# Half of the top-k counts moved from VectorE to GpSimd and ScalarE in a two-layer sparse-attention and retention trunk

## The chip, the cores and the metric

The kernel runs on one core of a Trainium2 chip. Its metric is device time in microseconds (us) of one execution. The engines named below are TensorE (PE), VectorE (DVE), ScalarE (ACT), GpSimd (POOL) and SyncE (SP, which issues the DMAs); each works through its own list of instructions in order.

## The reference, cut to what matters

Input and output are 1024 tokens of 1024 features, float32. Layer 0 is sparse attention: an indexer scores all keys, each query keeps the 256 best admissible keys, and attention runs over those. Layer 1 is retention. A gated convolutional feed-forward layer follows each.

```python
def block(args):                          # 8 blocks of 128 queries
    qb, qib, wb, tb = args
    limit = (tb // CHUNK + 1) * CHUNK
    admissible = key_pos[None, :] < limit[:, None]
    rel = relu(einsum('bqhd,bsd->bqhs', qib, ki))
    score = einsum('bqhs,bqh->bqs', rel, wb)
    score = where(admissible[None], score, -inf)
    _, idx = lax.top_k(score, 256)
    logits = einsum('bqhd,bqkd->bqhk', qb, gather(k, idx))
    p = softmax(where(valid, logits, -inf))
    return einsum('bqhk,bqkd->bqhd', p, gather(c, idx))
y = concat(blocks) @ w_out                # then conv_ffn, then retention, then conv_ffn
```

## The kernel before, in words

Every float32 product is made of three matmul passes over a high and a low part: `whi`/`wlo` for weights (L87 on ACT, L89 on DVE or, where the table of weights says so, on POOL), `hh`/`hl` and `qh`/`ql` for inputs. `bank` is one PSUM bank of 512 columns. A weight is fetched into `wraw` and split two weights ahead; three `whi`/`wlo` buffers go round.

Layer 0 is worked in two halves of four query blocks of 128. Block b has 128(b+1) keys, so blocks 0 and 1 need no top-k, blocks 2 to 7 have 384, 512, 640, 768, 896 and 1024 keys. The order is: `in_proj(0)`; the indexer for blocks 2 and 3 (relu on ACT, L385 adds the heads on DVE into `sc`); `in_proj(1)` with the indexer for blocks 4 to 7 inside it; attention for blocks 0 to 3; `out_proj(0)`; the first products of the feed-forward layer (`first_products`, 17 of the 22 chunks, copied out by ACT at L787); attention for blocks 4 to 7; `out_proj(1)`; the rest of the feed-forward layer.

The top-k finds each query's 256th largest score bit by bit. A count (L405) compares a block's scores with the threshold `tkt` and adds up the ones in `tkc`; two small steps turn the counts into the next threshold (L415, L416) and one keeps the best so far (L417). There are 33 counts for each block. Then L422 to L428 turn `sc` into an additive mask (a scan ranks ties). Two such searches exist: one for blocks 2 and 3, one for blocks 4 to 7; each works on all its blocks in one round. Their steps are generators, called by `steps(n)` between the pieces of other work.

Attention is made in groups of four heads. `att_probs` makes scores with the mask added and the row maximum (L484), the exponent's bias (L489), the exponential on ACT (L491), the reciprocal of its sum (L474) and the scaling on POOL (L475). `att_values` transposes the probabilities on PE (L512) and multiplies. One group is prepared ahead of the values.

The order within each engine's list is made by a scheduler when the kernel is built, which takes the program's order as the priority; it is fixed before the kernel runs.

Of the kernel before, what the change touches and what calls it, by code (L numbers as in the profile page):

```python
# [51 lines left out]
class Prog:  # L52
# [59 lines left out]
    def small(self, n, dt=F32):  # L112
        return self.sp.tile([128, n], dt, tag=f"s{n}", bufs=6 if n <= 8 else 2, name=f"s{n}")
# [102 lines left out]
    def in_proj(self, half, hh, hl, steps, also=lambda j, q, qs: None):  # L216
# [42 lines left out]
        for j in range(4):  # L259
            pq = self.proj_T(hh, hl, q0)  # L260
            sq = squares(pq[:, q0:])
            self.later(1, lambda j=j, sq=sq: sums(pms[:10, q0:], ea(2 + j), sq, False, j == 3))
            th, tl = self.tmp(F32R), self.tmp(F32R)
            self.split_psum(th[:, q0:], tl[:, q0:], pq[:, q0:], self.col(C_GQI))
            for (dst, src) in ((qs[0:64, 2 * j], th[0:64, q0:]), (qs[64:128, 2 * j], tl[0:64, q0:]),
                               (qs[0:64, 2 * j + 1], tl[64:128, q0:]), (qs[64:128, 2 * j + 1], th[64:128, q0:])):
                nc.sync.dma_start(dst.bitcast(F32), src.bitcast(F32))
            steps((2, 10)[half])
# [56 lines left out]
        self.later((4, 3)[half], idx_keys)  # L325
# [65 lines left out]
    def topk(self, scs, scratch):  # L391
# [3 lines left out]
        V = self.nc.vector  # L395
        B = len(scs)
        Ls = [sc.shape[1] for sc in scs]
        sml = lambda n, dt=F32: self.stat.tile([128, B], dt, tag=f"k{n}{B}", name=f"tk{n}")
        cnt, need = sml("c"), sml("n")
        best, bit, thr = sml("s", I32), sml("b", I32), sml("t", I32)  # L400
# [9 lines left out]
        yield from count(lambda b: 0.0, ALU.is_ge)  # L410
        V.tensor_scalar(best, cnt, TOPK - 0.5, -1.0, op0=ALU.is_lt, op1=ALU.mult)
        V.tensor_scalar(thr, best, 1 << 30, None, op0=ALU.bitwise_xor)
# [5 lines left out]
        yield from count(lambda b: t[:, b:b + 1], ALU.is_gt)  # L418
        V.tensor_scalar(need, cnt, -1.0, float(TOPK), op0=ALU.mult, op1=ALU.add)
        for b in range(B):  # L420
            nth, eq = scratch[:, 0, :Ls[b]], scratch[:, 1, :Ls[b]]
            V.tensor_scalar(eq, scs[b], t[:, b:b + 1], None, op0=ALU.is_equal)  # L422
            V.tensor_tensor_scan(nth, eq, eq, 0.0, ALU.add, ALU.max)
            yield
            V.scalar_tensor_tensor(eq, nth, need[:, b:b + 1], eq, op0=ALU.is_le, op1=ALU.mult)
            yield
            V.scalar_tensor_tensor(scs[b], scs[b], t[:, b:b + 1], eq, op0=ALU.is_gt, op1=ALU.add)
            V.tensor_scalar(scs[b], scs[b], -1.0, -MASKED, op0=ALU.add, op1=ALU.mult)  # L428
            yield

    def attention(self, blocks, q, masks, get_ot):

        items = [(b, g) for b in blocks for g in range(2)]
        nxt = self.att_probs(*items[0], q, masks)
        for _ in nxt:
            yield
        for n, (b, g) in enumerate(items):
            lg = self.lg
            ahead = self.att_probs(*items[n + 1], q, masks) if n + 1 < len(items) else iter(())
            nk = b + 1  # L440
            done = 0
            for j, _ in enumerate(self.att_values(b, g, lg, *get_ot())):
                while done < 5 and done * (nk + 1) < AHEAD * (j + 1):
                    next(ahead, None)
                    done += 1
                yield
            for _ in ahead:
                pass

    def att_probs(self, b, g, q, masks):  # L450
# [13 lines left out]
        else:  # L464
            if b == 0 and g == 0:
# [4 lines left out]
        last = None  # L470

        def normalise(i, sm):
            rs = self.small(1)
            nc.vector.reciprocal(rs, sm)  # L474
            nc.gpsimd.tensor_scalar(lg[:, i, :nk * 128], lg[:, i, :nk * 128], rs, 1.0, op0=ALU.mult, op1=ALU.mult)  # L475

        for i in range(4):
            h = 4 * g + i
            mx = []
            for (o, n) in self.segs(L):  # L480
                ps = self.bank()
                self.mm3(ps[:, :n], qh[:, h], ql[:, h], self.kTh[:, o:o + n], self.kTl[:, o:o + n], True, True)
                m = self.small(1)
                nc.vector.tensor_tensor_reduce(lg[:, i, o:o + n], ps[:, :n], mask[:, o:o + n], 1.0,  # L484
                                               mx[-1] if mx else INADM, ALU.add, ALU.max, m)
                mx.append(m)
            s = self.sq[:, b, h:h + 1]
            nm = self.small(1)
            nc.vector.scalar_tensor_tensor(nm, mx[-1], -1.0, s, op0=ALU.mult, op1=ALU.mult)  # L489
            sm = self.small(1)  # L490
            nc.scalar.activation(lg[:, i], lg[:, i], AF.Exp, bias=nm, scale=s, accum_out=sm)  # L491
            if last:
                normalise(*last)
            last = (i, sm)
            yield
        normalise(*last)
        yield

# [64 lines left out]
    def retention(self, half, x, h=None, then=None, also=lambda n: None):  # L563
        nc = self.nc
        hh, hl = h or self.all_chunks(x, C_GMIX + 8)
        kz = self.stat.tile([128, 4, 4], F32, tag="kz", name="kz")
        kn = self.stat.tile([128, 4, 4], F32, tag="kn", name="kn")
        ke = self.stat.tile([128, 4, 4], F32, tag="ke", name="ke")
# [237 lines left out]
    def second_inputs(self, x0, x1, tt, chunk):  # L806
# [3 lines left out]
        for k in (0, 2):  # L810
# [3 lines left out]
            self.split(two(T1, 0, k), two(T1, 1, k), two(x0, k))  # L814
        for k in range(4):
# [22 lines left out]
    def ffn_first(self, x, tt, s3):  # L838
# [5 lines left out]
        nxt = self.prep_b(0, 0, self.up_raw(0, 0), s3)  # L844
        T1, T2, T4, B22, T3 = self.second_inputs(x0, x1, tt, chunk)
# [45 lines left out]
    def ffn_whole(self, l, x):  # L891
# [38 lines left out]
        nxt = self.prep_b(l, 0, wa[0][0], s3)  # L930
        T1, T2, T4, B22, T3 = self.second_inputs(x0, x1, tt, chunk)
# [125 lines left out]
    def run(self):  # L1057
# [5 lines left out]
        with ExitStack() as es:  # L1063
# [27 lines left out]
            with tc.tile_pool(name="og0", bufs=2, reuse_waits="tile") as self.ogp, \  # L1091
# [54 lines left out]
                q0, qs0 = self.in_proj(0, *h0[:2], steps)  # L1146
                steps(100)
                self.sc = l0.tile([128, 4224], F32, tag="sc", name="sc")
                for b in (2, 3):
                    for _ in self.indexer(b, qs0, (b - 2) * 128, masks):  # L1150
                        pass
                    self.flush(self.nproj + b - 1)
                self.mean_square(1)
                scratch = l0.tile([128, 2, 1024], F16, name="scratch")
                gens.append(self.topk([masks[2], masks[3]], scratch))
                idx = []

                def index(j, q, qs):
                    if j == IDX_FROM:
                        idx.append((None for b in (4, 5, 6, 7) for _ in self.indexer(b, qs, (b - 4) * 128, masks)))  # L1160
                    if j >= IDX_FROM:
                        for _ in range(-(-32 // (8 - IDX_FROM))):
                            next(idx[0], None)

                q1, qs1 = self.in_proj(1, *h1[:2], steps, index)
# [13 lines left out]
                for _ in self.first_products(range(NFF - PRE[0]), B):  # L1179
                    steps(3)  # L1180
# [120 lines left out]
```

## Time and profile before

| | |
|---|---|
| median of 3 runs | 2787.89 us (2786.62 to 2789.54) |
| the profiled execution | 2782.56 us, span 2780.8 us |
| PE busy | 2654.3 us (95%) |
| DVE busy | 1881.0 us (68%) |
| ACT busy | 1090.9 us (39%) |
| POOL busy | 264.9 us (10%) |

How to read it: the page divides the span in 40 slices. PE stands at 9 tenths in nearly all of them after the first ten, so the stretch in which PE is not full is the first quarter, up to some 713 us. There DVE shows 9 tenths in the slices from about 140 to 560 us, while PE shows 7 and 6. PEclk, the clock that TensorE was granted, falls to 7 tenths in the slices where PE waits most. POOL works almost only in that first quarter.

### The profile page before, as it was taken

Reading aid. Unit: us, or ns where it says so; the run is one execution under the profiler, and the core shown is the slowest. Engines: PE = TensorE matmul, PEld = TensorE weight load, DVE = VectorE, ACT = ScalarE, POOL = GpSimd, SP = SyncE. Lnnn points to the kernel's source line nnn. Section 1 sums busy time; section 2 is a strip of 40 time slices with the busy share of each in tenths; the row PEclk is TensorE's granted clock in tenths of the full one; section 3 lists DMA queues with packets and bytes.
Section 4 is the critical chain, followed back from the end, with each engine's and each line's share of the span. In section 5 each row is a group of like instructions: output and inputs, shape, how many; then the busy total and the mean of one; then the engine's idle time right before and its main releaser. Section 6 shows DMA issues by size and latency. Waiting matters only on the chain.

```text
span 2780.8 us, 31488 instructions
## 1 busy us (share of the span) xinstructions
PE 2654.3 (95%) x11888; PEld 2175.0 (78%) x11888; DVE 1881.0 (68%) x2928; ACT 1090.9 (39%) x1546; POOL 264.9 (10%) x193
## 2 busy tenths in 40 slices
PE   8977679998999999999999999999998999999999
PEld 6755568787788878888888888888886888888887
DVE  5699999975987878744444445445447977777632
ACT  6435423563433333323333333323334554544210
POOL 2443234321000000000000000000000000000000
PEclk9988789999999999999999999999999999999999
DMA  6220025304466575412222224222222432337722
GB/s 196 71 78 23 31 91 172 116 5 152 163 200 195 195 257 177 152 61 96 84 77 90 91 77 128 76 82 92 80 73 90 144 106 106 120 108 288 232 59 87
DMA packets 110344, 328.35 MB, mean 118 GB/s; under 512 B 12400, under 2 KB 13808, under 8 KB 110192
## 3 DMA queue, kind: packets, MB, share of 16 engines
q1 hardware_dynamic: 110192, 326.34, 35.7%
q8 instruction: 93, 1.52, 0.2%
q14 instruction: 59, 0.48, 0.1%
HBM read 250.27 MB, written 72.35 MB: 116 GB/s over the span
## 4 chain that ended last, share of the span: by engine, by line
PE 77%; DVE 4%; DMA 2%; ACT 1%; issue 1%; POOL 0%; SPq 0%; DVEq 0%; ACTq 0%
PE bank L731 28%; PE bank L123 16%; PE bank L125 16%; PE bank L124 16%; PE bank L512 1%; DMA gin<-ud 1%; DMA wraw<-in_wf_up 1%; DVE T L709 1%; DVE xo L742 1%; DVE wlo L709 1%; PE bank L688 0%; DVE t L742 0%; DVE x L717 0%; DMA ud<-cu 0%; DVE gin L742 0%
## 5 line engine op out<-in xcount | busy, mean ns | idle before, releaser
L87 ACT ACTIVATE whi<-wraw 128x1024 fp32r<-128x1024 f32 (+1 forms) x194 | 204.9, 1056 | 510.3 <-PE bank L124 263.0
L731 PE MATMUL bank<-T,whi 128*128 128x512 f32 x1072 | 336.8, 395 | 21.9 <-ACT T L708 14.8
L731 PE MATMUL bank<-B,whi 128*128 128x512 f32 x1056 | 326.4, 392 | 7.7 <-DVE B L709 4.0
L89 DVE TENSOR_TENSOR wlo<-wraw,whi 128x1024 fp32r<-128x1024 f32 (+1 forms) x151 | 184.6, 1224 | 209.0 <-ACT whi L87 207.9
L124 PE MATMUL bank<-g,whi 128*128 128x512 f32 x704 | 273.6, 389 | 0.0
L125 PE MATMUL bank<-g,wlo 128*128 128x512 f32 x704 | 272.1, 389 | 0.5 <-DVE wlo L709 0.5
L123 PE MATMUL bank<-g,whi 128*128 128x512 f32 x704 | 265.5, 390 | 5.6 <-ACT g L708 4.6
L731 PEld LDWEIGHTS bank<-T,whi 128*128 128x128 f32 x1072 | 203.9, 190 | 70.4 <-ACT T L708 16.5
L708 ACT ACTIVATE whi<-wraw 128x1024 fp32r<-128x1024 f32 (+2 forms) x153 | 144.8, 947 | 269.3 <-PE bank L124 133.6
L731 PEld LDWEIGHTS bank<-B,whi 128*128 128x128 f32 x1056 | 198.8, 189 | 50.5 <-DVE B L709 5.0
L709 DVE TENSOR_TENSOR wlo<-wraw,whi 128x1024 fp32r<-128x1024 f32 (+2 forms) x153 | 165.2, 1080 | 76.0 <-ACT whi L708 75.9
L731 PE MATMUL bank<-T,wlo 128*128 128x512 f32 x536 | 210.4, 394 | 0.0
L731 PE MATMUL bank<-B,wlo 128*128 128x512 f32 x528 | 204.1, 390 | 0.0
L123 PE MATMUL bank<-hh,whi 128*128 128x512 f32 (+2 forms) x480 | 188.6, 393 | 11.3 <-ACT hh L134 8.9
L124 PE MATMUL bank<-wlo,hh 128*128 128x512 f32 x512 | 199.3, 389 | 0.0
L125 PE MATMUL bank<-whi,hl 128*128 128x512 f32 x512 | 199.2, 389 | 0.0
L123 PE MATMUL bank<-whi,hh 128*128 128x512 f32 x512 | 198.9, 390 | 0.0
L124 PE MATMUL bank<-hl,whi 128*128 128x512 f32 (+2 forms) x480 | 186.5, 389 | 0.1
L125 PE MATMUL bank<-hh,wlo 128*128 128x512 f32 (+2 forms) x480 | 186.0, 388 | 0.0
L405 DVE TENSOR_SCALAR_CACHE_REDUCE scratch<-sc,tkt 128x640 f16<-128x640 f32 (+1 forms) x192 | 180.7, 941 | 2.4
L742 DVE TENSOR_TENSOR xo<-xo,bank 128x512 f32<-128x512 f32 x128 | 86.5, 683 | 127.8 <-PE bank L125 127.6
L123 PEld LDWEIGHTS bank<-g,whi 128*128 128x128 f32 x704 | 132.0, 188 | 34.3 <-ACT g L708 5.4
(245 smaller groups left out, 5334.5 us busy)
## 6 DMA issues: line engine op xcount, KB each, us to landing
wraw<-in_wf_up SPq DMA_DIRECT2D x113, 512.0 KB, 3.6
ud<-cu SPq DMA_DIRECT2D x88, 512.0 KB, 2.6
gin<-ud SPq DMA_DIRECT2D x88, 512.0 KB, 4.4
wraw<-in_wb_vg SPq DMA_DIRECT2D x64, 512.0 KB, 3.5
wraw<-in_wf_dn SPq DMA_DIRECT2D x48, 384.0 KB, 3.5
wraw<-in_wb_qk SPq DMA_DIRECT2D x32, 512.0 KB, 3.5
wraw<-in_wb_out SPq DMA_DIRECT2D x32, 512.0 KB, 3.4
wraw<-in_wa_in SPq DMA_DIRECT2D x26, 512.0 KB, 3.9
```

The lines of the kernel that those rows point to most:

```text
L87: nc.scalar.activation(hi[:, :n], raw[:, :n], AF.Copy)
L89: eng.tensor_tensor(lo[:, :n], raw[:, :n], hi[:, :n].bitcast(F32), ALU.subtract)
L123: mm(ps, ah, bh, start=first, stop=False)
L124: mm(ps, ah, bl, start=False, stop=False)
L125: mm(ps, al, bh, start=False, stop=last)
L405: V.tensor_scalar(scratch[:, 0, :Ls[b]], scs[b], of(b), None, op0=op, op1=ALU.add, accum_out=cnt[:, b:b + 1])
L512: nc.tensor.transpose(pt[:, i * 128:(i + 1) * 128], lg[:, i, j * 128:(j + 1) * 128], self.ident)
L708: return (self.nc.scalar.activation(hi, raw, AF.Copy), self.nc.vector.tensor_tensor(lo, raw, hi.bitcast(F32), ALU.subtract))
L709: self.nc.vector.tensor_tensor(lo, raw, hi.bitcast(F32), ALU.subtract))
L731: self.nc.tensor.matmul(ps, u, v, start=first and k + i == 0, stop=k == 3 and i == 2, skip_group_check=not (first and last))
L742: self.nc.vector.tensor_tensor(o, a, b, op)
```

## The change

- The top-k works in pairs of blocks: a = (3, 2), b = (4, 5), c = (7, 6). Of each pair the first block is counted on DVE as before (`near`); the second on POOL, which writes the comparison as ones and zeros (`far`), and on ACT, which adds them up. Pair b and pair c are separate generators.
- The best value is no longer kept apart: the threshold itself carries it, with one small step less in each round. The comparison for ties goes to POOL, the last mask step to ACT.
- The indexer for blocks 2 and 3 runs inside `in_proj(0)`, so pair a starts earlier.
- Attention for blocks 0 to 3 calls no `steps`, and prepares up to two groups ahead. For blocks 4 to 7 the bias and the reciprocal are made for two heads at once.
- `wlo` of the 22 `wf_up` weights goes from POOL to DVE; in the feed-forward layer's start the first convolution's preparation is issued after the first two splits; `out_proj(0)` and `first_products` call fewer steps.

```diff
             elif ph == "up":
-                seq += [(i["wf_up"][0, c], 1024, True) for c in range(*a)]
+                seq += [(i["wf_up"][0, c], 1024, False) for c in range(*a)]
...
-            for b in range(B):
-                V.tensor_scalar(scratch[:, 0, :Ls[b]], scs[b], of(b), None, op0=op, op1=ALU.add,
-                                accum_out=cnt[:, b:b + 1])
-                yield
+            nc.gpsimd.tensor_scalar(far[:, :Ls[1]], scs[1], of(1), 1.0, op0=op, op1=ALU.mult)
+            nc.scalar.activation(far[:, :Ls[1]], far[:, :Ls[1]], AF.Copy, accum_out=cnt[:, 1:2])
+            V.tensor_scalar(near[:, :Ls[0]], scs[0], of(0), None, op0=op, op1=ALU.add, accum_out=cnt[:, 0:1])
...
         for k in range(30, -1, -1):
-            yield from count(lambda b: t[:, b:b + 1], ALU.is_ge)
-            V.tensor_scalar(bit, cnt, TOPK - 0.5, float(1 << k), op0=ALU.is_ge, op1=ALU.mult)
-            V.scalar_tensor_tensor(thr, bit, (1 << k) >> 1, best, op0=ALU.bitwise_xor, op1=ALU.bitwise_xor)
-            V.tensor_tensor(best, best, bit, ALU.bitwise_xor)
+            count(lambda b: t[:, b:b + 1], ALU.is_ge)
+            yield
+            V.tensor_scalar(bit, cnt, TOPK - 0.5, float(1 << k), op0=ALU.is_lt, op1=ALU.mult)
+            V.scalar_tensor_tensor(thr, bit, (1 << k) >> 1, thr, op0=ALU.bitwise_xor, op1=ALU.bitwise_xor)
...
-            V.tensor_scalar(eq, scs[b], t[:, b:b + 1], None, op0=ALU.is_equal)
+            nc.gpsimd.tensor_scalar(eq, scs[b], t[:, b:b + 1], 1.0, op0=ALU.is_equal, op1=ALU.mult)
...
-            V.tensor_scalar(scs[b], scs[b], -1.0, -MASKED, op0=ALU.add, op1=ALU.mult)
+            nc.scalar.activation(scs[b], scs[b], AF.Copy, bias=MASKED, scale=-MASKED)
...
+            upto = 5 * min(n + 1 + (2 if b < 3 else 1), len(items))
...
-        nxt = self.prep_b(0, 0, self.up_raw(0, 0), s3)
-        T1, T2, T4, B22, T3 = self.second_inputs(x0, x1, tt, chunk)
+        T1, T2, T4, B22, T3 = self.second_inputs(x0, x1, tt, chunk, lambda: nxt.append(
+            self.prep_b(0, 0, self.up_raw(0, 0), s3)))
...
-                gens.append(self.topk([masks[2], masks[3]], scratch))
+                q0, qs0 = self.in_proj(0, *h0[:2], steps, index((2, 3)))
+                gens.append(self.topk("a", [masks[3], masks[2]], near, far[0]))
+                q1, qs1 = self.in_proj(1, *h1[:2], steps, index((4, 5, 6, 7)))
                 steps(200)
-                gens.append(self.topk([masks[b] for b in (4, 5, 6, 7)], scratch))
+                gens.append(self.topk("b", [masks[4], masks[5]], near, far[0]))
+                gens.append(self.topk("c", [masks[7], masks[6]], near, far[1]))
                 for _ in self.attention(range(4), q0, masks, get_ot):
-                    steps(1)
-                x[0] = self.out_proj(0, *ot, lambda m: steps(5))
+                    pass
+                x[0] = self.out_proj(0, *ot, lambda m: steps(2))
...
                 for _ in self.first_products(range(NFF - PRE[0]), B):
-                    steps(3)
+                    steps(2)
                 steps(200)
                 for _ in self.attention(range(4, 8), q1, masks, get_ot):
```

How the lists of instructions differ at three places. The first is DVE in attention for blocks 0 to 3, around the second head group of block 2. Before (L405 is a count, L484 the scores, L489 the bias, L474 the reciprocal, L132 the low part of a bank):

```order
L489 SCALAR_TENSOR_TENSOR s1_2784<-s1_2782,sq_89 128x1
L417 TENSOR_TENSOR tks_2388<-tks_2388,tkb_2389 128x4
L405 TENSOR_SCALAR scratch_1161,tkc_2386<-sc_1041,tkt_2390 128x640
L474 RECIPROCAL s1_2788<-s1_2776 128x1
L484 ISA lg2_2375,s1_2795<-bank_2791,sc_1041 128x384
L484 ISA s1_2795 128x1
L132 TENSOR_TENSOR t2_2811<-bank_2805,t2_2810 128x512
L405 TENSOR_SCALAR scratch_1161,tkc_2386<-sc_1041,tkt_2390 128x768
L132 TENSOR_TENSOR t2_2840<-bank_2834,t2_2839 128x512
L489 SCALAR_TENSOR_TENSOR s1_2797<-s1_2795,sq_89 128x1
```

Now, at the same groups (L498 the scores, L507 the bias, L511 the reciprocal):

```order
L498 ISA lg2_2637,s1_2728<-bank_2729,sc_848 128x384
L498 ISA s1_2728 128x1
L132 TENSOR_TENSOR otl_2443<-bank_2707,oth_2442 128x4x128
L507 SCALAR_TENSOR_TENSOR s1_2734<-s1_2728,sq_89 128x1
L511 RECIPROCAL s1_2725<-s1_2724 128x1
L498 ISA lg2_2637,s1_2741<-bank_2742,sc_848 128x384
L498 ISA s1_2741 128x1
L507 SCALAR_TENSOR_TENSOR s1_2747<-s1_2741,sq_89 128x1
L511 RECIPROCAL s1_2736<-s1_2735 128x1
L498 ISA lg2_2637,s1_2754<-bank_2755,sc_848 128x384
```

The 13 rounds over four blocks that stood here have become six rounds of the pairs b and c, all in blocks 2 and 3, and the last six rounds of pair a in blocks 0 and 1. The second place is POOL in the projections of `in_proj(1)`. Before (L233 is a step of the squares for the norms):

```order
L89 TENSOR_TENSOR wlo_1440<-wraw_1438,whi_1439 128x1024
L233 TENSOR_TENSOR t2_1401<-t2_1399,t2_1400 128x512
L89 TENSOR_TENSOR wlo_1512<-wraw_1510,whi_1511 128x1024
L233 TENSOR_TENSOR t2_1473<-t2_1471,t2_1472 128x512
L89 TENSOR_TENSOR wlo_1587<-wraw_1585,whi_1586 128x1024
```

Now (L406 is the comparison for a far count, L139 the power for the norms):

```order
L406 TENSOR_SCALAR far768_356<-sc_848,tkt_1194 128x384
L89 TENSOR_TENSOR wlo_1616<-wraw_1614,whi_1615 128x1024
L233 TENSOR_TENSOR t2_1599<-t2_1597,t2_1598 128x512
L406 TENSOR_SCALAR far768_356<-sc_848,tkt_1194 128x384
L89 TENSOR_TENSOR wlo_1657<-wraw_1655,whi_1656 128x1024
```

Nearly each weight split now has a comparison ahead of it that waits for DVE's threshold. The third place is DVE at the end of `first_products`. Before, the end of the mask for block 7, the next weight, and the first scores of block 4:

```order
L422 TENSOR_SCALAR scratch_1161<-sc_1041,tkt_2390 128x1024
L423 SCALAR_TENSOR_TENSOR scratch_1161<-scratch_1161 128x1024
L425 SCALAR_TENSOR_TENSOR scratch_1161<-scratch_1161,tkn_2387 128x1024
L427 SCALAR_TENSOR_TENSOR sc_1041<-sc_1041,tkt_2390,scratch_1161 128x1024
L428 TENSOR_SCALAR sc_1041<-sc_1041 128x1024
L89 TENSOR_TENSOR wlo_4203<-wraw_4201,whi_4202 128x1024
L484 ISA lg_4294,s1_4299<-bank_4295,sc_1041 128x384
```

Now, at the last weight that the products need (`tkc_3119` and `tkt_3122` belong to pair b, `tkc_3126` and `tkt_3129` to pair c; L408 is the near count, L419 and L420 the two small steps):

```order
L89 TENSOR_TENSOR wlo_4350<-wraw_4348,whi_4349 128x1024
L419 TENSOR_SCALAR tkb_3121<-tkc_3119 128x2
L420 SCALAR_TENSOR_TENSOR tkt_3122<-tkb_3121,tkt_3122 128x2
L408 TENSOR_SCALAR near_355,tkc_3119<-sc_848,tkt_3122 128x640
L89 TENSOR_TENSOR wlo_5579<-wraw_5577,whi_5578 128x1024
L408 TENSOR_SCALAR near_355,tkc_3126<-sc_848,tkt_3129 128x1024
L419 TENSOR_SCALAR tkb_3128<-tkc_3126 128x2
L420 SCALAR_TENSOR_TENSOR tkt_3129<-tkb_3128,tkt_3129 128x2
L419 TENSOR_SCALAR tkb_3121<-tkc_3119 128x2
```

From there DVE's list holds nothing but rounds until the search ends; ACT's list has 18 far counts (nine of each pair) behind its last copy of a product, and PE's has only the scores of block 4. Behind the last round stand the masks of blocks 4 and 7, then the first scores, and between these the masks of blocks 5 and 6:

```order
L423 TENSOR_SCALAR tkn_3127<-tkc_3126 128x2
L423 TENSOR_SCALAR tkn_3120<-tkc_3119 128x2
L431 SCALAR_TENSOR_TENSOR rank_4236<-rank_4236 128x640
L433 SCALAR_TENSOR_TENSOR rank_4236<-rank_4236,tkn_3120 128x640
L435 SCALAR_TENSOR_TENSOR sc_848<-sc_848,tkt_3122,rank_4236 128x640
```

The search's last nine rounds and its ends have moved from beside the products to behind them.

## Rows read from the trace of the kernel before

**Rows 1.** Windows by stage: busy us (instructions) by engine; PEclk, DMA share, GB/s.
```profile
100.00:181.00 81.00, 66.08 (x282) 50.95 (x280) 77.03 (x190) 28.84 (x43) 49.23 (x23) 0.93 0.33 95
181.00:252.00 71.00, 57.92 (x247) 43.36 (x247) 70.27 (x146) 43.25 (x88) 22.01 (x11) 0.91 0.10 30
252.00:364.00 112.00, 76.89 (x279) 56.03 (x280) 107.93 (x320) 43.38 (x97) 33.24 (x38) 0.71 0.06 19
...
416.00:512.00 96.00, 96.00 (x424) 79.80 (x425) 92.22 (x159) 36.00 (x52) 37.17 (x14) 0.98 0.52 170
512.00:525.00 13.00, 10.17 (x58) 7.68 (x57) 11.49 (x38) 8.76 (x18) 7.16 (x7) 1.00 0.38 124
...
672.00:713.00 41.00, 28.69 (x107) 20.37 (x105) 36.23 (x46) 18.38 (x24) 0.73 (x1) 0.88 0.30 99
```

**Rows 2.** Timeline of DVE: start us, duration; two successive rounds' first count.
```profile
441.45 0.87 DVE L405 TENSOR_SCALAR_CACHE_REDUCE scratch<-sc,tkt 128x640 f16<-128x640 f32 x1
...
446.42 0.87 DVE L405 TENSOR_SCALAR_CACHE_REDUCE scratch<-sc,tkt 128x640 f16<-128x640 f32 x1
```

**Rows 3.** Groups of DVE by form: busy us, mean ns of one, idle before.
```profile
L405 DVE TENSOR_SCALAR_CACHE_REDUCE scratch<-sc,tkt 128x1024 f16<-128x1024 f32 x32 | 40.8, 1276 | 0.5
...
L405 DVE TENSOR_SCALAR_CACHE_REDUCE scratch<-sc,tkt 128x640 f16<-128x640 f32 x32 | 27.9, 872 | 0.0
...
L405 DVE TENSOR_SCALAR_CACHE_REDUCE scratch<-sc,tkt 128x384 f16<-128x384 f32 x32 | 19.4, 605 | 0.0
```

**Rows 4.** Groups of POOL by form, the same columns.
```profile
L89 POOL TENSOR_TENSOR wlo<-wraw,whi 128x1024 fp32r<-128x1024 f32 x43 | 107.0, 2488 | 187.6 <-ACT whi L87 158.5 <-PE bank L225 22.0 <-PE bank L731 6.0
...
L475 POOL TENSOR_SCALAR lg<-lg,s 128x896 f32<-128x896 f32 x8 | 8.2, 1019 | 15.3 <-DVE s L474 9.1 <-PE bank L512 4.2 <-ACT t L131 2.0
L475 POOL TENSOR_SCALAR lg<-lg,s 128x768 f32<-128x768 f32 x8 | 7.3, 910 | 14.5 <-DVE s L474 9.9 <-PE bank L124 4.6
...
L475 POOL TENSOR_SCALAR lg<-lg,s 128x384 f32<-128x384 f32 x8 | 4.7, 588 | 19.6 <-DVE s L474 12.7 <-DVE tkt L416 4.2 <-PE bank L512 2.7
```

**Rows 5.** Groups of ACT by form, the same columns.
```profile
L491 ACT ACTIVATION_READ_ACCUMULATOR lg<-lg,s,sq 128x1 f32 x64 | 12.0, 188 | 0.0
...
L491 ACT ACTIVATE lg<-lg,s,sq 128x896 f32<-128x896 f32 x8 | 9.1, 1136 | 2.3 <-DVE s L474 2.2
L491 ACT ACTIVATE lg<-lg,s,sq 128x768 f32<-128x768 f32 x8 | 8.2, 1026 | 5.0 <-DVE s L474 2.9 <-DVE s L489 2.1
```

**Rows 6.** Timeline of DVE where a POOL instruction runs beside it.
```profile
106.67 2.42 DVE L411 TENSOR_SCALAR tks<-tkc 128x2 int32<-128x2 f32 x1
...
111.03 0.75 DVE L405 TENSOR_SCALAR_CACHE_REDUCE scratch<-sc,tkt 128x512 f16<-128x512 f32 x1
...
111.81 1.99 DVE L415 TENSOR_SCALAR tkb<-tkc 128x2 int32<-128x2 f32 x1
```

**Rows 7.** Timeline of POOL in the same stretch.
```profile
106.66 2.40 POOL L89 TENSOR_TENSOR wlo<-wraw,whi 128x1024 fp32r<-128x1024 f32 x1
...
111.38 2.40 POOL L89 TENSOR_TENSOR wlo<-wraw,whi 128x1024 fp32r<-128x1024 f32 x1 [1.07 <-ACT whi L87]
```

**Rows 8.** Timeline of DVE: small steps, block 7's mask, block 4's first scores.
```profile
436.00 0.17 DVE L415 TENSOR_SCALAR tkb<-tkc 128x4 int32<-128x4 f32 x1
436.21 0.16 DVE L416 SCALAR_TENSOR_TENSOR tkt<-tkb,tks 128x4 int32<-128x4 int32 x1
...
501.14 2.29 DVE L423 TENSOR_TENSOR_SCAN scratch<-scratch 128x1024 f16<-128x1024 f16 x1
503.47 1.28 DVE L425 SCALAR_TENSOR_TENSOR scratch<-scratch,tkn 128x1024 f16<-128x1024 f16 x1
...
507.85 0.55 DVE L484 CUSTOM_DVE_ANT_0 lg<-bank,sc 128x384 f32<-128x384 f32 x1
```

**Rows 9.** Timeline of PE: block 4's first transpose.
```profile
513.51 0.33 PE L512 MATMUL bank<-kon,lg 128*128 128x128 f32 x1 [0.52 <-POOL lg L475]
```

**Rows 10.** Waits of DVE, 672 to 690 us: us, times, longest.
```profile
DVE t L742 <- DMA wraw<-in_wf_up: 15.3, 1, 15.3
```

More of the change, by code (lines that the diff above doesn't have):

```diff
@@ new lines, in topk @@
+        count(lambda b: t[:, b:b + 1], ALU.is_gt)
+        yield
+        V.tensor_scalar(need, cnt, -1.0, float(TOPK), op0=ALU.mult, op1=ALU.add)
+        rank = near, far
+        if max(Ls) > 512:
+            r = self.k4.tile([128, 2, 1024], F16, tag="k4", name="rank")
+            rank = r[:, 0], r[:, 1]
+        for b in (0, 1):
+            nth, eq = rank[0][:, :Ls[b]], rank[1][:, :Ls[b]]
+            nc.gpsimd.tensor_scalar(eq, scs[b], t[:, b:b + 1], 1.0, op0=ALU.is_equal, op1=ALU.mult)
@@ L433, in attention, with probs @@
         items = [(b, g) for b in blocks for g in range(2)]
-        nxt = self.att_probs(*items[0], q, masks)
-        for _ in nxt:
+        lgs = []
+        def probs():
+            for b, g in items:
+                yield from self.att_probs(b, g, q, masks)
+                lgs.append(self.lg)
+        ahead = probs()
+        for _ in range(5):
+            next(ahead)
             yield
+        made = 5
         for n, (b, g) in enumerate(items):
-            lg = self.lg
-            ahead = self.att_probs(*items[n + 1], q, masks) if n + 1 < len(items) else iter(())
+            while len(lgs) <= n:
+                if next(ahead, 0) == 0:
+                    break
+                made += 1
             nk = b + 1
-            done = 0
-            for j, _ in enumerate(self.att_values(b, g, lg, *get_ot())):
-                while done < 5 and done * (nk + 1) < AHEAD * (j + 1):
+            upto = 5 * min(n + 1 + (2 if b < 3 else 1), len(items))
+            done, m0 = 0, made
+            for j, _ in enumerate(self.att_values(b, g, lgs[n], *get_ot())):
+                while made < upto and (made - m0) * (nk + 1) < AHEAD * (j + 1):
                     next(ahead, None)
-                    done += 1
+                    made += 1
                 yield
-            for _ in ahead:
-                pass
+            while made < 5 * min(n + 2, len(items)):
+                next(ahead, None)
+                made += 1
     def att_probs(self, b, g, q, masks):
@@ L469, in att_probs, with scores @@
         self.lg = lg
[L470 to L477, printed above, removed]
+        def scores(i, ms):
             h = 4 * g + i
-            mx = []
-            for (o, n) in self.segs(L):
+            last = INADM
+            for (o, n), m in zip(self.segs(L), ms):
                 ps = self.bank()
@@ L490, in att_probs, with probs @@
[L490 to L497, printed above, removed]
+                nc.vector.tensor_tensor_reduce(lg[:, i, o:o + n], ps[:, :n], mask[:, o:o + n], 1.0, last,
+                                               ALU.add, ALU.max, m)
+                last = m
+        def probs(hs, mx):
+            n = len(hs)
+            s = self.sq[:, b, 4 * g + hs[0]:4 * g + hs[0] + n]
+            nm, sm, rs = self.small(n), self.small(n), self.small(n)
+            nc.vector.scalar_tensor_tensor(nm, mx, -1.0, s, op0=ALU.mult, op1=ALU.mult)
+            for j, i in enumerate(hs):
+                nc.scalar.activation(lg[:, i], lg[:, i], AF.Exp, bias=nm[:, j:j + 1], scale=s[:, j:j + 1],
+                                     accum_out=sm[:, j:j + 1])
+            return lambda: (nc.vector.reciprocal(rs, sm), [nc.gpsimd.tensor_scalar(
+                lg[:, i, :nk * 128], lg[:, i, :nk * 128], rs[:, j:j + 1], 1.0, op0=ALU.mult, op1=ALU.mult)
+                for j, i in enumerate(hs)])
@@ L499, in att_values @@
+        group = 2 if b >= 4 else 1
+        last = lambda: None
+        for i in range(4):
+            if i % group == 0:
+                mx = [self.small(group) for _ in self.segs(L)]
+            scores(i, [m[:, i % group:i % group + 1] for m in mx])
+            if i % group == group - 1:
+                now = probs(list(range(i + 1 - group, i + 1)), mx[-1])
+                last()
+                last = now
+            yield 1
+        last()
+        yield 1
     def att_values(self, b, g, lg, oth, otl):
@@ L1156, in run @@
[L1156 to L1165, printed above, removed]
+                near = l0.tile([128, 1024], F16, name="near")
@@ new lines, in run, with index, also @@
+                far = [l0.tile([128, n], F16, name=f"far{n}") for n in (768, 896)]
+                def index(blocks):
+                    idx = []
+                    def also(j, q, qs):
+                        if j == IDX_FROM:
+                            if blocks[0] == 2:
+                                steps(100)
+                                self.sc = l0.tile([128, 4224], F32, tag="sc", name="sc")
+                            idx.append((None for b in blocks
+                                        for _ in self.indexer(b, qs, (b - blocks[0]) * 128, masks)))
+                        if j >= IDX_FROM:
+                            for _ in range(-(-8 * len(blocks) // (8 - IDX_FROM))):
+                                next(idx[0], None)
+                    return also
```

59 lines of the change are left out of this document (24 added, 35 removed).

## The prediction, made before the changed kernel ran

> **What bounds the kernel now.** I read the page's slices first: PE is full after some 713 us, where the change only reorders, so all that can be won or lost lies before. The windows by stage come next [rows 1]; there PE's busy time times its granted clock is about what the stage's matmuls need at full clock, and the rest of the stage is loss. For the projections of `in_proj(1)` (100 to 181 us) that is 66.1 x 0.93 = 61.5 of 81; for the indexer of blocks 4 to 7 (181 to 252) 52.7 of 71; for attention of blocks 0 to 3 (252 to 364) 54.6 of 112; for the first products (416 to 512) 94 of 96. In the first three stages DVE is busy for 255 of 264 us: DVE sets their length, and PE loses 95 us there. In the products DVE is just as busy (92 of 96) but PE is full: there the counts cost nothing. So the same count is worth its whole length in one stage and nothing in another. The timelines then give the price of each piece: one round over four blocks takes 446.42 - 441.45 = 4.97 us [rows 2].
>
> **The change part by part: what is won.** Attention of blocks 0 to 3 loses 13 such rounds, 64.6 us of DVE. It gains six rounds of the pairs b and c. Of one, DVE keeps two near counts (0.87 and 1.28) [rows 3], two reads of the sum (0.08 each) and four small steps at a pitch of 0.2 [rows 8], 3.1 us; six are 19. It also gains six rounds of pair a (0.75 + 0.08 + 0.4 = 1.2 each [rows 6, 8], 7), the masks of blocks 2 and 3 (4) and the first counts (2). DVE is left with 107.9 - 64.6 + 32 = 75, against PE's 54.6. With waits between the engines I take 87, so 25 us won; the bounds are 17 (95 us, a fifth of it waits) and 33 (79 us, DVE nearly gapless).
>
> In the projections of `in_proj(1)` DVE loses the 384-column counts (0.6 each [rows 3]) and a third small step. But POOL was busy 49.2 us there and gets some 20 comparisons of 384 columns, at 0.59 us by the scaling of that width [rows 4]: 61, as much as PE's 61.5. Two engines at their limit that feed each other leak, so I take 69: 12 won (6 to 18). In the indexer stage pair a finishes later but lighter; DVE's 70.3 falls to some 57, PE needs 52.7, and ACT, which is in the search's chain now, has 43 us of its own ahead of the counts. I take 4 (0 to 11).
>
> The start of the feed-forward layer (672 to 713) loses 41 - 25 = 16 us. One wait of DVE for the first `wf_up` weights stands in it, 15.3 us [rows 10], and the normaliser and the first splits are queued behind it on DVE. The change issues them ahead of it. The DMA itself comes no earlier, so I take 6 of it (0 to 10). `out_proj(0)` and the products stay: `wlo` of 22 weights moves to DVE, 1.2 us each, and DVE loses more in counts than that; this is hidden under full PE. If ACT's counts hold up its weight splits, that cover is thin, but the third buffer for `whi` and `wlo` gives a weight's time of slack. The fewer small steps in blocks 4 to 7 lie beside PE that is full already (zero). Won in all: 25 + 12 + 4 + 6 = 47 us, bounds 23 and 72.
>
> **What is paid.** The rounds that left attention have to go somewhere. Five fit in `out_proj(0)` and the gap behind it, thirteen beside the products. By the changed list nine rounds of each pair stand behind the last weight of the products, with nothing on PE's list but the scores of block 4. In the trace before, the whole search was over at 507.85 us while PE had products until 512, and the first transpose came at 513.51 [rows 8, 9].
>
> The price of a round there is in no row. From below it is DVE's own 3.1 us; ACT needs less (1.03 + 1.14 + twice 0.19 = 2.55, with the exponentials of those widths as prices [rows 5]), POOL too (0.91 + 1.02 at the price of the scaling [rows 4]). But the parts wait for each other. A small step of DVE that meets a running POOL instruction waits for its end: L411 started at 106.67 beside a weight split of POOL from 106.66 to 109.06 and took 2.42 us, and L415 took 1.99 until the next one ended, while a count beside it took its normal 0.75 [rows 6, 7]. In a round the pair-c small step follows directly on the pair-b threshold that lets POOL start, so it waits for POOL's 0.91. With 0.2 for handing ACT's sum over: 3.1 + 0.91 + 0.2 = 4.2 us. From above, the comparison might run at the rate of POOL's two-input operation, 2488 ns for 1024 columns, so 1.87 for 768: 5.2 us. I take 4.2, since the scaling is also one instruction with one tensor and two scalar operands.
>
> [...]
>
> [...]
>
> Nine rounds are 38 us (28 to 47). Behind them come the masks of blocks 4 and 7: scan and two steps at 1024 columns are 2.29 + 1.28 + 1.28 = 4.85 [rows 8], for 640 by width 3.0, together 7.9. Then the first scores wait with the masks of blocks 5 and 6 among them (another 7.9, and 4.5 of scores) before the reciprocal that POOL's scaling and the first transpose need: 12.4, where it was 5.7 before. PE does some 4 us of scores in that time, and 2.8 us were lost around there already (512 to 525 [rows 1]). So 38 + 7.9 + 12.4 - 4 - 2.8 = 51.5, and 2 for the clock, which stood at 0.71 in the stage where PE waits most [rows 1] and will be low when PE starts again: 53 us, bounds 41 and 66.
>
> **The sum.** 53 - 47 = 6 us longer than the profiled execution's 2782.6, so 2788.6. The median of the runs is 5.3 us above that execution (2787.9), so I predict 2794 us, 0.2% slower.
>
> **The rivals.**
> *The relief carries and the tail is short (faster).* Attention runs at 78 us, the projections at 64, the indexer stage at 60, the start of the feed-forward layer wins 8: 34 + 17 + 11 + 8 = 70. For it speaks that DVE shows hardly any idle time in the three stages, so that it alone may have been the brake; against it that POOL has as much to do as PE in the projections. With the tail at 48 this gives 2766.
> *The two cancel (no change).* Round price 3.65 (the small steps meet POOL only in part) makes the tail 48, the win is 47: 2789. What speaks for it is that the two sums are within 6 us of each other on bounds of 25 each.
> *The comparison is slow on POOL (clearly slower).* At 2.4 ns a column POOL has 49.2 + 20 x 0.93 = 68 us in the projections, which then win 6 at most; the round takes 5.2, the tail 62; attention and indexer win 24, and the feed-forward start 6. The time is 62 - 36 = 26 longer: 2814. It decides from about 1.5 ns a column on. For it speaks that the only other elementwise POOL work in the trace goes at that rate; against it the scaling's 1.1 ns.
> *The new waits starve PE (slower).* POOL's weight splits now stand behind comparisons that wait for a threshold, which waits for ACT's sum, which stands behind weight copies on ACT. If that ring is longer than the slack of the buffers, the projections win nothing and the products stop now and then: 12 + 6 more than my sum, 2812. Against it: the splits are made two weights ahead.
>
> **Chances.** My forecast (a few us to about 15 slower) 0.30; relief carries 0.32; the two cancel 0.20; slow comparison 0.12; starving 0.06. What a measurement of this kernel can tell from no change is about 0.2%, 5.6 us. Faster by more than that is the first rival, 0.32; within it the second, 0.20; slower the rest, 0.48. For the range I go from the faster rival with a little more (2762) to the slow comparison with a little more (2824); the bounds 23 to 72 and 41 to 66 taken all one way would reach 2757 and 2831. The forecast's own range is 2789 to 2803.
>
> **What the profile after would show.** Right: attention of blocks 0 to 3 takes 79 to 95 us with DVE still the busiest; a stretch of some 35 to 45 us behind the last copy of a product in which PE does nothing, POOL, ACT and DVE hand rounds on at 3.7 to 4.7 us each, and another 20 us before the first transpose; far comparisons at 0.9 to 1.0 us for 768 and 896 columns. Wrong: comparisons above 1.5 us (then slower), DVE gapless and PE's clock at full in attention (then faster), products with gaps before their weights, or nine rounds that end under products.

## The result, and the profile after

The changed kernel takes 2856.64 us (median of 4 runs, 2855.35 to 2856.93) against 2787.26 for the kernel before beside it: 1.0249 times as long, 95% interval 1.0236 to 1.0262. I had said 2794, 0.2% slower; it is 2.5% slower. The side was right, the size was not.

The two kernels compared by landmarks in the traces; each column is the length of a stage in us:

| stage, from and to | before | after | difference | predicted |
|---|---|---|---|---|
| start to the first scores of attention | 252.3 | 241.3 | -11.0 | -16 |
| attention of blocks 0 to 3, to the first add of `out_proj(0)` | 112.1 | 99.7 | -12.4 | -25 |
| `out_proj(0)` and the gap, until the products run | 51.4 | 59.6 | +8.2 | 0 |
| products and what is behind them, to block 4's first transpose | 97.7 | 172.6 | +74.9 | +53 |
| to the last add of `out_proj(1)` | 141.3 | 142.8 | +1.5 | 0 |
| the feed-forward layer's first dozen chunks | | | +8 | -6 |

The last row is the distance between the same convolution steps in the two traces, which grows from 61 us at the end of `out_proj(1)` to 69 at the thirteenth step; from there on it grows by 1 us up to the 25th, and by another 3 up to the end (the two spans differ by 73.8 us).

The windows of after by stage answer to [rows 1] (busy us of PE, PEld, DVE, ACT and POOL with their instructions, then PEclk, DMA share, GB/s):

```profile
100.00:181.00 81.00, 68.15 (x295) 51.72 (x294) 42.03 (x79) 39.59 (x78) 73.07 (x40) 0.89 0.36 101
181.00:241.00 60.00, 53.85 (x230) 41.73 (x229) 53.92 (x97) 43.91 (x99) 37.93 (x21) 0.89 0.10 28
241.30:341.00 99.70, 67.35 (x281) 51.78 (x282) 81.03 (x252) 57.60 (x140) 80.06 (x58) 0.78 0.07 26
341.00:400.60 59.60, 39.74 (x162) 31.70 (x161) 44.33 (x70) 28.50 (x45) 53.67 (x19) 0.81 0.32 106
400.60:495.00 94.40, 94.39 (x405) 77.60 (x405) 62.62 (x117) 55.64 (x97) 74.19 (x24) 0.97 0.54 175
495.00:573.20 78.20, 9.11 (x30) 8.12 (x30) 49.67 (x102) 27.35 (x51) 69.62 (x24) 0.54 0.06 18
```

DVE is no longer full (54 of 60 us at the most), and POOL nearly is: 73 of 81 us in the projections, 80 of 100 in attention, 54 of 60 in the gap. In the sixth row PE is busy for 9 of 78 us. The groups of POOL by form say why; they answer to [rows 4], where the scaling of 896 columns took 1019 ns:

```profile
L406 POOL TENSOR_SCALAR far<-sc,tkt 128x896 f16<-128x896 f32 x32 | 106.4, 3326 | 18.5 <-DVE tkt L420 16.1 <-ACT far L407 1.1 <-DVE s L511 1.0
L406 POOL TENSOR_SCALAR far<-sc,tkt 128x768 f16<-128x768 f32 x32 | 93.5, 2922 | 12.5 <-DVE tkt L420 12.5
L406 POOL TENSOR_SCALAR far<-sc,tkt 128x384 f16<-128x384 f32 x32 | 51.7, 1616 | 29.7 <-DVE tkt L420 14.5 <-ACT t L380 9.9 <-DVE tkt L415 2.8
```

The comparison takes 3.7 ns a column at 896 columns and 4.2 at 384. I had taken 1.1 and as my upper end 2.4. The stretch behind the products in three timelines of after, first PE (the last product, block 4's first scores, its first transpose):

```profile
494.60 0.39 PE L761 MATMUL bank<-B,wlo 128*128 128x512 f32 x1
543.59 0.69 PE L123 MATMUL bank<-kTh,qh 128*128 128x384 f32 x1 [48.60 <-ACT qh L479]
573.23 0.48 PE L542 MATMUL bank<-kon,lg 128*128 128x128 f32 x1 [8.65 <-POOL lg L511]
```

then POOL, whose comparisons there stand without a gap and are drawn as one row:

```profile
499.02 48.69 POOL L406 TENSOR_SCALAR far<-sc,tkt 128x896 f16<-128x896 f32 x16 [1.08 <-ACT far L407]
```

and DVE over one round:

```profile
506.61 0.88 DVE L408 TENSOR_SCALAR_CACHE_REDUCE near<-sc,tkt 128x640 f16<-128x640 f32 x1
507.54 1.28 DVE L408 TENSOR_SCALAR_CACHE_REDUCE near<-sc,tkt 128x1024 f16<-128x1024 f32 x1
509.51 0.17 DVE L419 TENSOR_SCALAR tkb<-tkc 128x2 int32<-128x2 f32 x1 [0.68 <-ACT far L407]
509.78 0.16 DVE L420 SCALAR_TENSOR_TENSOR tkt<-tkb,tkt 128x2 int32<-128x2 int32 x1
512.23 0.17 DVE L419 TENSOR_SCALAR tkb<-tkc 128x2 int32<-128x2 f32 x1 [2.29 <-ACT far L407]
512.70 0.88 DVE L408 TENSOR_SCALAR_CACHE_REDUCE near<-sc,tkt 128x640 f16<-128x640 f32 x1
```

A round takes 512.70 - 506.61 = 6.09 us, exactly two of POOL's sixteen comparisons (48.69 / 8). DVE waits 3 of the 6 us. Both small steps take their normal 0.17 us although POOL runs all the time.

### The profile page after: what moved, and what is told of

The parts are those of the page before. It is cut to its first block, busy times and chain, and to the rows that moved or that the text cites. A ratio compares the mean times of both kernels' runs of the same rounds, so it can differ in the third digit from the quotient of the medians.

```text
span 2854.6 us, 31750 instructions
## 1 busy us (share of the span) xinstructions
PE 2657.2 (93%) x11888; PEld 2177.9 (76%) x11888; DVE 1819.5 (64%) x2711; ACT 1174.5 (41%) x1750; POOL 485.6 (17%) x276
## 4 chain that ended last, share of the span: by engine, by line
PE 79%; DVE 10%; DMA 3%; issue 3%; ACT 3%; POOL 2%; SPq 0%; DVEq 0%; ACTq 0%; POOLq 0%
PE bank L761 25%; PE bank L123 17%; PE bank L124 17%; PE bank L125 17%; POOL far L406 1%; DMA wraw<-in_wf_up 1%; DMA gin<-ud 1%; PE bank L542 1%; DVE near L408 1%; DVE sc L385 1%; DVE wlo L739 1%; DVE T L739 1%; DVE xo L772 1%; DVE wraw L772 0%; DVE t L772 0%
## 5 line engine op out<-in xcount | busy, mean ns | idle before, releaser
L89 DVE TENSOR_TENSOR wlo<-wraw,whi 128x1024 fp32r<-128x1024 f32 (+1 forms) x173 | 214.7, 1242 | 241.4 <-ACT whi L87 240.0
L406 POOL TENSOR_SCALAR far<-sc,tkt 128x896 f16<-128x896 f32 (+1 forms) x96 | 251.1, 2622 | 60.8 <-DVE tkt L420 43.1
```

Source lines behind the costliest of these rows:

```text
L89: eng.tensor_tensor(lo[:, :n], raw[:, :n], hi[:, :n].bitcast(F32), ALU.subtract)
L406: nc.gpsimd.tensor_scalar(far[:, :Ls[1]], scs[1], of(1), 1.0, op0=op, op1=ALU.mult)
```

## The experiments

Three theories were tried against each other. P: the price of POOL's comparison makes the loss. O (and C): the hand-overs, or the summed cost of the search, make it. H, which came only after the second experiment: it matters where the scheduler puts the rounds, since a round that is ready fills every gap in DVE's list. All times are medians, with the ratio to the kernel before beside them and its 95% interval.

**e1_cheap_far.** The comparison becomes two multiplications and the threshold stays where it started, so the kernel leaves the top-k out but keeps its instructions and waits.

```diff
-            nc.gpsimd.tensor_scalar(far[:, :Ls[1]], scs[1], of(1), 1.0, op0=op, op1=ALU.mult)
+            nc.gpsimd.tensor_scalar(far[:, :Ls[1]], scs[1], 0.0, of(1), op0=ALU.mult, op1=ALU.mult)
```

> The far comparison on POOL is replaced by two multiplications of the same block into the same tile, and the small steps leave the threshold where it started, so the masks are not those of a top-k; every instruction, wait and hand-over of a round is still there. Theory P (the price of POOL's comparison, 2.9 and 3.3 us for 768 and 896 columns, makes the loss): the operation takes about 0.9 and 1.0 us, the list holds no rounds behind the products any more, block 4's first transpose comes at about 470 us instead of 573, and the time is 2725 to 2765 us, faster than before. Theory O (the hand-overs between POOL, ACT and DVE make the loss, at whatever price): the operation is cheap but the time stays above 2800. Theory F (it is the float16 output, not the comparison, that is slow on POOL): the operation still takes 2.9 and 3.3 us and the time stays at 2857.

Measured: 2790.26 us, 1.0014 (1.0005 to 1.0024). Groups of POOL, then the window of attention:

```profile
L406 POOL TENSOR_SCALAR far<-sc,tkt 128x896 f16<-128x896 f32 x32 | 33.2, 1038 | 19.4 <-DVE tkt L420 7.4 <-ACT far L407 3.4 <-DVE s L511 2.9
```
```profile
247.60:350.20 102.60, 75.07 (x284) 52.49 (x285) 98.98 (x323) 74.44 (x171) 63.25 (x73) 0.78 0.06 21
```

Same shape, same float16 output, 1038 instead of 3326 ns: theory F falls, and it is the comparison that is slow. Which of the two scalars is the column `tkt` has no part in it: the search's first count, which compares with the constant 0, takes 3724 ns for 896 columns in the changed kernel, and the multiplication in its place 1317. The time falls by 66 us, so O falls too; this is price and place together, since the lists are made anew for each kernel. But P's number is missed by 25 us: no rounds are left behind the products, and still the kernel is no faster than before. The list shows where they went: the scheduler put 20 of 33 rounds into attention, where DVE is full again (99 of 103 us).

**e2_far_on_dve.** All counts on DVE, the rest of the change kept.

```diff
-            nc.gpsimd.tensor_scalar(far[:, :Ls[1]], scs[1], of(1), 1.0, op0=op, op1=ALU.mult)
-            nc.scalar.activation(far[:, :Ls[1]], far[:, :Ls[1]], AF.Copy, accum_out=cnt[:, 1:2])
+            V.tensor_scalar(far[:, :Ls[1]], scs[1], of(1), None, op0=op, op1=ALU.add, accum_out=cnt[:, 1:2])
```

> The far counts and the comparison for ties go back to DVE in one instruction each; pairs, fewer small steps, the indexer of blocks 2 and 3 inside the first projection and the rest of the change stay. Theory P: the rest of the change is no loss, the time is 2765 to 2800 us, around that of before, with attention of blocks 0 to 3 again set by DVE. Theory O': the moved steps (no rounds called in attention, fewer in the products) are what puts rounds behind the products, so 2815 or more.

Measured: 2861.16 us, 1.0269 (1.0254 to 1.0285). P's range is missed. The time lies where O' had it (2815 or more), but not for its reason: as slow as the change, with nothing behind the products. The window of attention:

```profile
247.90:409.60 161.70, 94.12 (x292) 64.41 (x293) 161.63 (x491) 44.29 (x97) 30.67 (x37) 0.59 0.04 13
```

28 of 33 rounds stand in attention, which takes 161.7 us with DVE full. A scheduler that fills each gap with what is ready would take a count of about a microsecond just before the attention's next step becomes ready. The steps that called the rounds in `out_proj(0)` and the products did not keep them there. That is theory H.

**e6_prep_first** and **e5_up_on_pool** undo two small parts.

```diff
-        T1, T2, T4, B22, T3 = self.second_inputs(x0, x1, tt, chunk, lambda: nxt.append(
-            self.prep_b(0, 0, self.up_raw(0, 0), s3)))
+        nxt = self.prep_b(0, 0, self.up_raw(0, 0), s3)
+        T1, T2, T4, B22, T3 = self.second_inputs(x0, x1, tt, chunk, lambda: None)
```

> Only the order in the feed-forward layer's start is undone (the first convolution's preparation is issued first, as before). Between the end of out_proj(1) and 795 us the changed kernel lost 11 us against before. If this reorder makes them, the time is 2843 to 2849 us; if it is the weight splits that moved to DVE, or the place where the search ended, it stays within 4 us of 2857.

Measured: 2855.81 us, the same as the change. The order of the preparation is worth nothing either way.

```diff
-                seq += [(i["wf_up"][0, c], 1024, False) for c in range(*a)]
+                seq += [(i["wf_up"][0, c], 1024, True) for c in range(*a)]
```

> Only the low parts of the 22 wf_up weights go back to POOL. Theory P (POOL is the bound of the search, full from the first products to the search's end): 17 splits of 2.4 us stand on POOL before the search's end, so the time is 20 to 45 us longer than the changed kernel's, 2875 to 2900, though the start of the feed-forward layer wins some us back. If POOL is not the bound there: 2846 to 2857.

Measured: 2898.09 us, 1.0402 (1.0387 to 1.0418). The 17 splits of 2.4 us are 41 us of POOL. The last comparison of the search ends 33 us later than in the changed kernel (580.9 against 547.7), and so do block 4's first scores (595.2 against 562.0): POOL is the bound of the search from the gap to its end. The other 8 us of the loss come after the search, so that 41 stands on both sides is chance.

**e3_sign_on_act, e4_sign_held, e2h_dve_held** test H. In the first, ACT alone counts the far block; in the other two, pairs b and c may not start before DVE's last scores of block 3.

```diff
+            nc.scalar.activation(far[:, :Ls[1]], scs[1], AF.Sign, bias=t[:, 1:2], scale=-1.0, accum_out=cnt[:, 1:2])
...
+        with self.tc.issue_after(self.hold[HOLD].ins) if tag != "a" else ExitStack():
+            exact(lambda b: 0.0, ALU.is_ge)
```

> As the changed kernel, but a far count is one ACT instruction (the sign of threshold minus score, with its sum), so POOL has no part in the search; the first and the last far count of a block and the comparison for ties are DVE's. In its list 28 of the 33 rounds of pairs b and c stand in attention of blocks 0 to 3, as in e2_far_on_dve, and none beside the products. Theory H (rounds that are always ready are put into every gap of DVE and hold up the attention's own steps; where they stand matters more than what they cost): attention takes about 125 us, the time is 2800 to 2835 us, slower than before although the search is cheaper. Theory C (what counts is the cost of the search on each engine): with 3.3 us of DVE a round instead of 5, the time is 2745 to 2775.

> The same counts by ACT, but pairs b and c may not start before DVE has made block 3's last scores, and the low parts of the wf_up weights are POOL's again, as before. In its list 8 rounds stand at the end of attention, 13 in out_proj(0), 13 beside the products, none behind them. Theory H: attention of blocks 0 to 3 falls from 112 us (before) to 75 to 88, the products stay full, the time is 2740 to 2770 us, faster than before and than e3_sign_on_act by 40 or more. Theory C: within 15 us of e3_sign_on_act.

> e2_far_on_dve (all counts on DVE), with pairs b and c held until DVE has made block 3's last scores. In its list 5 rounds stand in attention, 7 in out_proj(0), 21 beside and some four behind the products, with the masks behind these. Theory H: attention falls from 162 us to 75 to 90; the rounds behind the products and the masks cost some 35 us there; the time is 2785 to 2825, against 2861 without the hold. Theory C: 2850 to 2870, since the same instructions are run.

Measured: 2794.34 (1.0025, 1.0015 to 1.0035), 2754.85 (0.9883, 0.9869 to 0.9898) and 2811.82 us (1.009, 1.0075 to 1.0105). The first misses its range by 6 us (attention took 111, not 125). The other two times lie in their ranges; e4_sign_held gets more out of attention than expected (70 us, not 75 to 88) and is 39 us faster than e3_sign_on_act, where 40 or more was expected. The windows of attention, in this order of kernels:

```profile
240.50:351.60 111.10, 79.16 (x278) 55.50 (x279) 108.01 (x437) 93.03 (x204) 28.29 (x36) 0.71 0.06 20
```
```profile
239.10:309.30 70.20, 57.75 (x279) 44.28 (x279) 63.57 (x236) 51.94 (x120) 27.16 (x35) 0.93 0.09 31
```
```profile
248.70:324.10 75.40, 63.50 (x292) 48.70 (x292) 65.42 (x219) 41.58 (x97) 29.45 (x36) 0.89 0.08 29
```

Between the first and the second the counts are the same (the second has also the splits of `wf_up` on POOL, as before), and the time differs by 39 us; between e2_far_on_dve and e2h_dve_held the hold alone is worth 49. So the place of the rounds makes a difference at the same counts, as H has it, and C falls. That a round in a gap delays attention by more than its own time is not shown: from the first window to the second DVE has 44 us less to do and attention is 41 us shorter, and from e2_far_on_dve to e2h_dve_held it is 96 and 86. The second is 1.2% faster than the kernel before: a far count by ACT takes 1030 ns for 896 columns, and of its 33 rounds 8 stand at the end of attention and the others in the gap and beside the products.

**e5_far_held.** The same hold for the change as it is.

```diff
-        count(lambda b: 0.0, ALU.is_ge)
+        with self.tc.issue_after(self.hold[3, 1].ins) if tag != "a" else ExitStack():
+            V.tensor_scalar(near[:, :Ls[0]], scs[0], 0.0, None, op0=ALU.is_ge, op1=ALU.add, accum_out=cnt[:, 0:1])
```

> The changed kernel with its slow comparison on POOL, but pairs b and c held until DVE has made block 3's last scores. In its list 12 rounds of each pair stand behind the last weight of the products instead of nine, and three to four in attention instead of seven. Theory P (with a comparison at 3.6 ns a column a round takes POOL 6.1 us, and 33 rounds of it cannot be hidden wherever they stand): attention gets 10 to 25 us shorter, the stretch behind the products 15 to 25 longer, and the time stays within 15 us of 2857. If the place of the rounds alone made the loss, as between e3_sign_on_act and e4_sign_held, it falls by 35 or more, to 2822 or less.

Measured: 2868.99 us, 1.0297 (1.028 to 1.0315). Attention got 10.7 us shorter (89.0), the stage from the products to the transposes 21.9 longer. With the slow comparison this other place does not help: the rounds that leave attention come back behind the products.

```profile
477.60:578.60 101.00, 9.12 (x32) 8.12 (x32) 60.07 (x132) 35.11 (x67) 94.37 (x32) 0.54 0.05 16
```

**e6_mask_on_dve, e7_no_rank_tile** try to take more from e4_sign_held.

```diff
-            nc.scalar.activation(scs[b], scs[b], AF.Copy, bias=MASKED, scale=-MASKED)
+            V.tensor_scalar(scs[b], scs[b], -1.0, -MASKED, op0=ALU.add, op1=ALU.mult)
...
-        if max(Ls) > 512:
-            r = self.k4.tile([128, 2, 1024], F16, tag="k4", name="rank")
-            rank = r[:, 0], r[:, 1]
```

> e4_sign_held with the last mask step on DVE again instead of ACT. In e4_sign_held PE lost 10 us between 425 and 440 us, waiting for ACT's copies of the products; ACT's list has the mask steps ahead of these, and they wait for DVE's scans. If that is the reason, those waits go and the time is 2743 to 2751 us; if not, it stays at 2755.

> e6_mask_on_dve without the tile for the ranks that the scans took from the buffers in which attention keeps qh and ql; the scans use the counts' own tiles. In e6_mask_on_dve ACT stood 11.5 us at qh of block 4, which waits for DVE's last scans, with a weight and three copies of products behind it, and PE lost 10 us. If that is the reason, the wait goes and the time is 2741 to 2749 us; if PE then waits elsewhere for the same time, it stays at 2754.

Measured: 2754.19 and 2755.46 us; neither is faster than e4_sign_held, so of each expectation the second half holds. In e4_sign_held ACT did stand at the mask step (`L440`); with that step on DVE it stands at `qh` instead. ACT's timelines of e4_sign_held and of e6_mask_on_dve:

```profile
426.04 0.74 ACT L440 ACTIVATE sc<-sc 128x640 f32<-128x640 f32 x1 [9.21 <-DVE sc L439]
```
```profile
436.92 1.06 ACT L483 ACTIVATE qh<-q 128x1024 fp32r<-128x1024 f32 x1 [11.51 <-DVE sc L439]
```

Without the rank tile that wait is gone and the last add of `out_proj(1)` comes 13.4 us earlier (608.0 against 621.4), but the feed-forward layer's first dozen chunks give 9 us of it back, and its later ones the rest. DVE's waits for the weights' DMA from 608 to 800 us in e7_no_rank_tile, where e6_mask_on_dve has 15.7 us in three waits from 615 to 800:

```profile
DVE t L771 <- DMA wraw<-in_wf_up: 27.0, 6, 15.0
```

Why SP's list brings these weights later in some kernels was not tried.

## Why the prediction was wrong, point by point

**The step that failed: the price of a comparison on POOL.** I took the scaling's price because it has the same operands and let the two-input operation be the upper end. It is a third kind: 3326 ns where the multiplication of the same block takes 1038 (e1_cheap_far), and 1616 against 648 for 384 columns, so 3.2 times the multiplication's time at 896 columns. I gave a slow comparison one chance in eight, and at too low a price (2.4 ns a column, where 3.7 was measured at 896).

Of the 63 us between 2794 and 2857, some 22 lie behind the products, 13 in attention, 8 in the gap, 14 in the feed-forward layer and 5 ahead of attention. The price makes the first, as the rows show; it has a part in the second and third that was not measured by itself. With the price that I had assumed the kernel takes 2790 us (e1_cheap_far), close to my 2794, but that is luck: there no round stands behind the products, where I had 53 us, and attention takes 103 us, where I had 87.

**Behind the products: 53 said, 75 measured.** The place and the number of rounds were right (nine, from the changed list). The round took 6.09 us and not 4.2: from the end of the last product (494.99) to pair c's last small step (545.99) it is 51 us instead of 38. My working of the round was wrong besides: it added 0.91 us for a small step that waits for POOL, and the rows show none. From there to the first scores (562.00) it took 16 us, where I had 7.9 for the masks of blocks 4 and 7: pair b's last far count still ran until 548.7, the tie comparisons go at POOL's price (`L430` took 2.43 us for the 640 columns of block 4 and 3.70 for the 1024 of block 7), and DVE's own mask steps now meet POOL's work (`L435` took 3.28 us for the 640 columns of block 4 beside POOL's `ql`, and 1.28 for the 1024 of block 7). From the scores to the transposes it was 11.2 us against my 12.4.

**Attention: 25 said, 12 measured.** DVE was left with 81 us, near my 75 (I took out 13 rounds, where the trace of before has 14 whole ones in the stage), but POOL was busy for 80. The bounds (17 to 33) left the measured value out, because POOL's price was in none of them. It does not come in by the scaling: PE waits for that 0.7 us in the whole stage, where before it was 18.0. PE's longest wait is for the end of pair a's search:

```profile
287.11 0.69 PE L123 MATMUL bank<-kTh,qh 128*128 128x384 f32 x1 [10.32 <-DVE s L498]
```

Block 2's first scores need its mask. Seven counts of pair a stand in the stage, each with a comparison of 1.6 us on POOL, and behind them the tie comparisons of blocks 3 and 2 (2.0 and 1.6 us), for which DVE waits. The prediction had counted these rounds by DVE's time alone, with no wait for their end. In e1_cheap_far pair a's search is over before attention starts, which is 6 us later than here. What made the rest of the 12 us was not separated.

**The gap: nothing said, 8 lost.** There too POOL is busy for 54 of 60 us, with the weight splits of `out_proj(0)`, and PE waits 4.2 us for one of them (a `wlo`). But the stage is as long at the low price (59.3 us) and with POOL out of the search (59.2 in e3_sign_on_act), by another wait: PE stands 11.4 and 12.6 us for DVE's `acc` there, 6.6 in the changed kernel and 5.5 before. So the price is not needed for this loss; what would make the stage as short as before was not tried.

**The feed-forward layer: 6 won said, 8 lost.** e6_prep_first shows that the reorder is worth nothing. The loss is at the first dozen chunks, where DVE waits 8.2 us for the weights' DMA (810 to 880 us; 0.7 from 749 to 811 before); e1_cheap_far and e4_sign_held have none of it there (the first loses some 6 us later in the layer), e2_far_on_dve and e7_no_rank_tile do. That SP's list fetches them later is my best reason, but it is argued, not shown.

**What held.** The stretch ahead of attention is 11 us shorter (13 in e4_sign_held), of 16 said. With all counts on DVE (e2_far_on_dve) it is 4.4 us, so the moved indexer alone does not make the 11. Blocks 4 to 7 and the fewer small steps there are worth nothing, 1.5 us lost. And my first rival, relief of DVE in attention, is real and larger than I had it where the rounds are held out of the stage: e4_sign_held gets 42 us out of attention (112.1 to 70.2), against the 25 of my forecast and the 34 of that rival. What I did not see is that relief alone buys little where a scheduler fills the free time with whatever is ready (e1_cheap_far: attention 9.5 us shorter than before, 2790 us in all).

## What to carry to other kernels

Before work moves to another engine, ask for a row of that operation on that engine; where there is none, the nearest operation of the same shape is no bound (here 1038 ns for a multiplication and 3326 for a comparison of the same 896 columns). A search that is off the critical path belongs under the stage in which TensorE is full, and if a scheduler orders the lists, it has to be held there, since in attention, with DVE full, the rounds lengthened the stage by about their own time (from e2_far_on_dve to e2h_dve_held DVE had 96 us less to do and attention was 86 us shorter), while beside the products of the kernel before, where PE was busy for 96 of 96 us, the rounds cost PE nothing. And read the list of instructions for what stands behind the last piece of cover: nine rounds behind the products were to be seen before any run.

## What the runs showed of the hardware

- GpSimd compares float32 against a per-partition threshold at 3326 ns for 128x896 and 1616 ns for 128x384 (the changed kernel, L406); it multiplies the same blocks into the same float16 tile in 1038 and 648 ns (e1_cheap_far).
- VectorE's small steps took longer beside some GpSimd instructions than beside others. In the changed kernel L419 (128x2) took 0.16 us on average in the 30 cases that started beside none. In the seven that started beside one of POOL's weight splits (L89) it took 1.1 to 2.1 us, and in six of these it ended within 0.03 us of the split. Beside the scaling (L511) of 256 and 512 columns three took 0.25 to 0.40 us and ended with it too. Beside the comparison (L406) it took 0.15 to 0.86, with a mean of 0.32 over 45; in the unbroken run of comparisons all 15 took 0.17. VectorE's weight splits (128x1024) took 1.38 us on average in the 18 cases that started beside a comparison, and 1.22 beside none.
- The same small step one column wide (128x1) took 0.14 to 0.16 us in all 43 that started beside a weight split of POOL in e4_sign_held.
- ScalarE counts by the sign function and its sum in 1030 + 188 ns for 896 columns (e4_sign_held). In the changed kernel the comparison of 896 columns on GpSimd takes 3326 ns and the adding on ScalarE 946 + 193; VectorE needs 1139 + 82 for the whole count (e2_far_on_dve).
